# A weight block's low part written by two GpSimd instructions of half the block

## Chip, core and metric

The kernel runs on one core of one Trainium2 chip. The metric is the device time of one launch in microseconds (us), taken as the median of several runs. Engines are named as the profile names them: PE is TensorE's matmul, PEld its weight load, DVE VectorE, ACT ScalarE, POOL GpSimd, SP SyncE.

## What is computed

Two transformer-like blocks run one after the other on 1024 tokens of width 1024, all in float32. Cut to what matters:

```
h    = rms_norm(x) * (1 + sc1) + sh1                 # sc1, sh1 from c @ w_ada
p_u, p_v, p_q, p_k, p_val, p_qi, p_ki, p_wi = split(h @ w_in)
y_a  = spatial_gating(gelu(p_u), gelu(p_v))
y_b  = attention over the 256 keys of highest index score (top-k per query)
x    = x + g1 * rms_norm(concat(norm(y_a), norm(y_b)) @ w_out)
x    = x + g2 * rms_norm(square(relu(h2 @ w_ff1)) @ w_ff2)
...
z    = rms_norm(x) @ w_in_2                          # second block
y_a  = rwkv7_time_mix(z_mix);  y_b = s5_ssm(u)       # a recurrence, a state space
x    = x + (g_a * y_a + g_b * y_b) @ w_out_2
x    = x + square(relu(rms_norm(x) @ w_ff_up_2)) @ w_ff_down_2
return rms_norm(x)
```

## The kernel before, in words

Float32 precision is kept by splitting each operand of a large matmul in two float32r parts: `hi`, the rounded value, and `lo`, what is left. A product is then three matmuls (`mm3`, L66, L68 and L69): hi by hi, and the two mixed ones. So every weight that is loaded needs a `hi` and a `lo` before PE can use it.

`load_w` (L99) does that for one block of weights of 512 KB: one DMA on SP's queue brings it as `wraw` (128 partitions by `nk` row tiles by `n` columns, 1024 elements per partition in 410 blocks and 656 in 8), and `split` (L58) makes `hi` with a copy on ACT (L60) and `lo` with a subtraction on POOL (L61). Both lie in one tile `whl`. Three buffers of `wraw` and three of `whl` let the loads run ahead of PE. Two callers stream the blocks: `token_major` (two row tiles of 512 columns per block) and `feature_major` (four row tiles of 256 columns per block); `merge` calls it directly. The two products that need `lo` of the weights stand at L68 in `token_major` and at L69 in `feature_major`.

The order of each engine's instructions is fixed at build time: the framework's scheduler simulates the program in time and issues by priority. `urgent()` (L53) puts the splits and the reading out of PSUM first. Beside the large matmuls run the parts that live on DVE: the top-k selection (`topk_steps`, a loop of 31 counting steps per tile of 128 queries: the count at L665, one small step at L675 and one at L676 that combines two small tiles in SBUF), the attention (L731 to L775), the triangular solve of the recurrence (L1383 and L1385, 62 short operations per tile), the sums of the feed-forward part (L898). Index scores are made by PE at L631 and L632 from queries that DVE has split (L604), PE has transposed (L124, out of the tile `smr`).

Of the kernel before, what the change touches and what calls it, by code (L numbers as in the profile page):

```python
# [8 lines left out]
F32 = mybir.dt.float32  # L9
# [5 lines left out]
OP = mybir.AluOpType  # L15
# [19 lines left out]
class Kernel:  # L35
# [64 lines left out]
    def load_w(self, w, k0, nk, c0, n, spare=None):  # L100


        nc = self.nc
        for _ in range(2):
            next(self.background, None)
        raw = self.wraw.tile([P, 1024], F32, name="wraw")[:, :nk * n].rearrange("p (k n) -> p k n", n=n)
        nc.sync.dma_start(raw, w[k0 * P:(k0 + nk) * P, c0:c0 + n].rearrange("(k p) n -> p k n", p=P))
        if spare:
            hls = [spare.tile([P, 2, 512], F32R, name="hT") for k in range(nk)]
            for k, hl in enumerate(hls):  # L110
                self.split(hl[:, 0], hl[:, 1], raw[:, k, :])
            return [(hl[:, 0], hl[:, 1]) for hl in hls]
        hl = self.whl.tile([P, 2, 1024], F32R, name="whl")[:, :, :nk * n].rearrange("p a (k n) -> p a k n", n=n)
        self.split(hl[:, 0], hl[:, 1], raw)
        return [(hl[:, 0, k, :], hl[:, 1, k, :]) for k in range(nk)]

    def after(self, n, steps):
# [1749 lines left out]
```

## Time and profile before

| what | value |
|---|---|
| median of 3 runs | 3100.45 us (3094.46 to 3101.99) |
| profiled execution, own time | 3100.2 us |
| its span, first to last instruction | 3098.5 us |
| mean granted TensorE clock | 0.956 of full |
| PE / PEld busy | 92% / 76% |
| DVE / ACT / POOL busy | 59% / 40% / 44% |
| HBM traffic over the span | 119 GB/s |

Outside the span lie 1.7 us. The profiled execution stands 0.25 us under the median, so a sum made against it can be held against the median as it is. PE is the busiest engine in every stretch of the program; its idle time and the time at half clock are what is left to be had.

### The profile page before, as it was taken

Reading aid. Unit: us, or ns where it says so; the run is one execution under the profiler, and the core shown is the slowest. Engines: PE = TensorE matmul, PEld = TensorE weight load, DVE = VectorE, ACT = ScalarE, POOL = GpSimd, SP = SyncE. Lnnn points to the kernel's source line nnn. Section 1 sums busy time; section 2 is a strip of 40 time slices with the busy share of each in tenths; the row PEclk is TensorE's granted clock in tenths of the full one; section 3 lists DMA queues with packets and bytes.
Section 4 is the critical chain, followed back from the end, with each engine's and each line's share of the span. In section 5 each row is a group of like instructions: output and inputs, shape, how many; then the busy total and the mean of one; then the engine's idle time right before and its main releaser. Section 6 shows DMA issues by size and latency. Waiting matters only on the chain. (4 is left out here: it accounts for less than half of the span.)

```text
span 3098.5 us, 41775 instructions
## 1 busy us (share of the span) xinstructions
PE 2841.5 (92%) x15600; PEld 2342.0 (76%) x15600; DVE 1815.0 (59%) x3752; ACT 1249.3 (40%) x2123; POOL 1351.0 (44%) x867
## 2 busy tenths in 40 slices
PE   6977988898999898889899899998999999999998
PEld 5766777687787777668777778877777778888887
DVE  5699679999955944455573455533655643442222
ACT  4545555443444433334233334342343333343333
POOL 4565554443345643333333354442333434454444
PEclk9988999999999999999899999999999999999999
DMA  7445331222224455333224574653323234433332
GB/s 249 124 153 162 123 123 59 86 68 72 65 89 146 167 167 148 109 86 87 74 83 128 151 242 140 164 164 113 96 76 92 85 91 143 148 126 100 99 99 82
DMA packets 301499, 370.18 MB, mean 119 GB/s; under 512 B 70936, under 2 KB 209902, under 8 KB 301040
## 3 DMA queue, kind: packets, MB, share of 16 engines
q1 hardware_dynamic: 293296, 351.75, 37.3%
q10 hardware_dynamic: 8000, 15.76, 1.5%
q8 instruction: 123, 2.02, 0.3%
q14 instruction: 80, 0.66, 0.1%
HBM read 315.80 MB, written 51.65 MB: 119 GB/s over the span
## 5 line engine op out<-in xcount | busy, mean ns | idle before, releaser
L61 POOL TENSOR_TENSOR whl<-wraw,whl 128x1024 fp32r<-128x1024 f32 (+1 forms) x418 | 1025.2, 2460 | 1308.7 <-ACT whl L60 1221.3
L66 PE MATMUL mm<-hT,whl 128*128 128x512 f32 x1760 | 703.0, 400 | 29.2 <-DVE T L1385 5.7
L68 PE MATMUL mm<-hT,whl 128*128 128x512 f32 x1760 | 705.0, 401 | 0.0
L69 PE MATMUL mm<-hT,whl 128*128 128x512 f32 x1760 | 694.7, 398 | 4.7 <-POOL whl L61 4.7
L60 ACT CAST whl<-wraw 128x1024 fp32r<-128x1024 f32 (+1 forms) x418 | 434.8, 1042 | 609.1 <-PE mm L69 436.6
L66 PE MATMUL mm<-whl,hT 128*128 128x512 f32 (+1 forms) x1584 | 609.2, 402 | 50.4 <-DVE acc L898 28.0
L68 PE MATMUL mm<-whl,hT 128*128 128x512 f32 (+1 forms) x1584 | 625.6, 398 | 1.8 <-POOL whl L61 1.8
L69 PE MATMUL mm<-whl,hT 128*128 128x512 f32 (+1 forms) x1584 | 614.6, 397 | 0.4 <-DVE hT L61 0.4
L66 PEld LDWEIGHTS mm<-hT,whl 128*128 128x128 f32 x1760 | 337.2, 192 | 105.2 <-issue 13.4
L66 PEld LDWEIGHTS mm<-whl,hT 128*128 128x128 f32 x1584 | 305.8, 194 | 120.1 <-DVE acc L898 33.0
L69 PEld LDWEIGHTS mm<-hT,whl 128*128 128x128 f32 x1760 | 338.2, 192 | 75.9 <-POOL whl L61 6.4
L68 PEld LDWEIGHTS mm<-hT,whl 128*128 128x128 f32 x1760 | 337.9, 192 | 67.2 <-issue 0.9
L68 PEld LDWEIGHTS mm<-whl,hT 128*128 128x128 f32 x1584 | 306.1, 193 | 62.5 <-POOL whl L61 2.3
L69 PEld LDWEIGHTS mm<-whl,hT 128*128 128x128 f32 x1584 | 304.4, 193 | 62.1 <-DVE hT L61 1.0
L61 DVE TENSOR_TENSOR hT<-sm,hT 128x512 fp32r<-128x512 f32 x112 | 130.9, 1173 | 277.4 <-ACT hT L60 276.4
L898 DVE TENSOR_TENSOR acc<-mm,acc 128x512 f32<-128x512 f32 x240 | 162.2, 687 | 173.0 <-PE mm L69 172.8
L665 DVE TENSOR_SCALAR_CACHE_REDUCE junk<-score,topk 128x640 uint8<-128x640 f32 (+4 forms) x192 | 180.0, 940 | 1.8
L877 ACT ACTIVATE sm<-mm 128x512 f32<-128x512 f32 x128 | 76.5, 597 | 165.0 <-PE mm L69 163.6
L1383 DVE TENSOR_TENSOR Ttmp<-L,T 128x60 f32<-128x60 f32 (+24 forms) x248 | 78.4, 316 | 90.9 <-DMA L<-lt_d 83.5
L60 ACT CAST hT<-sm 128x512 fp32r<-128x512 f32 x144 | 89.4, 621 | 32.2 <-DVE sm L1831 28.7
L676 DVE SCALAR_TENSOR_TENSOR topk<-topk,topk 128x1 int32<-128x1 int32 x186 | 86.7, 469 | 1.3
L739 ACT ACTIVATE p<-p,nm 128x128 f32<-128x128 f32 (+7 forms) x64 | 49.5, 775 | 91.5 <-DVE nm L735 66.2
(471 smaller groups left out, 3495.3 us busy)
## 6 DMA issues: line engine op xcount, KB each, us to landing
wraw<-w_ff SPq DMA_DIRECT2D x128, 512.0 KB
wraw<-w_in SPq DMA_DIRECT2D x100, 512.0 KB
wraw<-w_ff_up SPq DMA_DIRECT2D x64, 512.0 KB
wraw<-w_ff_down SPq DMA_DIRECT2D x64, 512.0 KB
wraw<-w_ada SPq DMA_DIRECT2D x32, 512.0 KB
wraw<-w_out SPq DMA_DIRECT2D x32, 512.0 KB
raw<-w_ada SPq DMA_DIRECT2D x16, 512.0 KB
x_d<-acc ACTq DMA_DIRECT2D x16, 512.0 KB
```

Source lines behind the costliest of these rows:

```text
L60: self.nc.scalar.copy(hi, src)
L61: (engine or self.nc.gpsimd).tensor_tensor(lo, src, hi.bitcast(F32), op=OP.subtract)
L66: nc.tensor.matmul(ps, a[0], b[0], start=start, stop=False)
L68: nc.tensor.matmul(ps, a[0], b[1], start=False, stop=False)
L69: nc.tensor.matmul(ps, a[1], b[0], start=False, stop=stop)
L665: V.tensor_scalar(junk[:, :n], sel, value, 0.0, op0=op, op1=OP.add, accum_out=cnt)
L676: V.scalar_tensor_tensor(u, t, (1 << b) ^ (1 << b >> 1), keep, op0=OP.bitwise_xor, op1=OP.bitwise_xor)
L739: nc.scalar.activation(p[:, :n], p[:, :n], AF.Exp, bias=nm, scale=0.125, accum_out=su)
L877: nc.scalar.activation(r, ps, AF.Relu)
L898: nc.vector.tensor_tensor(d, pss[j], d, op=OP.add)
L1383: V.tensor_tensor(tmp[:, :n, :w], L[:, j:j + 1, j + 1:].to_broadcast([P, n, w]), T[:, :n, j:j + 1].to_broadcast([P, n, w]), op=OP.mult)
```

## The change

The branch of `load_w` that serves nearly all weights no longer calls `split`. It keeps the one ACT copy of the whole block and issues the subtraction as two POOL instructions, the first for the lower half of the row tiles, the second for the upper half. The branch for the last four tiles (`spare`) and all other splits stay.

```diff
         hl = self.whl.tile([P, 2, 1024], F32R, name="whl")[:, :, :nk * n].rearrange("p a (k n) -> p a k n", n=n)
-        self.split(hl[:, 0], hl[:, 1], raw)
+
+        with self.urgent():
+            nc.scalar.copy(hl[:, 0], raw)
+            for s in (slice(0, nk // 2), slice(nk // 2, nk)):
+                nc.gpsimd.tensor_tensor(hl[:, 1, s], raw[:, s], hl[:, 0, s].bitcast(F32), op=OP.subtract)
         return [(hl[:, 0, k, :], hl[:, 1, k, :]) for k in range(nk)]
```

Lines behind this place stand four lines lower in the changed kernel: L124 is then L128, L631 is L635, L898 is L902. The subtraction of a weight block is L118 there. The number of instructions is the same on every engine, but for the 418 further subtractions on POOL and two activation-table loads on ACT that fall away (30 instead of 32). The scheduler sees the two shorter subtractions, and so it moves other instructions.

On POOL, in the first feed-forward part beside the top-k selection (`whl` is a weight block, `hT` the feed-forward's activations, `smr` a split key tile), before:

```order
L582 TENSOR_TENSOR smr<-smS,smr 128x2x64
L583 COPY smr<-smr 128x2x64
L61 TENSOR_TENSOR whl<-wraw,whl 128x1024
L61 TENSOR_TENSOR hT<-sm,hT 128x512
L61 TENSOR_TENSOR whl<-wraw,whl 128x1024
L582 TENSOR_TENSOR smr<-smS,smr 128x2x64
L61 TENSOR_TENSOR hT<-sm,hT 128x512
L583 COPY smr<-smr 128x2x64
L61 TENSOR_TENSOR whl<-wraw,whl 128x1024 x5
```

and with the change:

```order
L586 TENSOR_TENSOR smr<-smS,smr 128x2x64 x2
L61 TENSOR_TENSOR hT<-sm,hT 128x512
L587 COPY smr<-smr 128x2x64 x2
L118 TENSOR_TENSOR whl<-wraw,whl 128x512 x2
L61 TENSOR_TENSOR hT<-sm,hT 128x512
L118 TENSOR_TENSOR whl<-wraw,whl 128x512 x2
L61 TENSOR_TENSOR hT<-sm,hT 128x512
L118 TENSOR_TENSOR whl<-wraw,whl 128x512 x10
```

The two halves of a block always stand next to each other; nothing of POOL's other work comes between them.

On PE, at the start of the product with `w_out` (`mm` with `hT` and `whl`), where the transposes of the next index-score queries (`tp` out of `smr`) are woven in, before:

```order
L66 MATMUL mm<-hT,whl 128x512
L68 MATMUL mm<-hT,whl 128x512
L124 MATMUL tp<-ident,smr 128x128 x8
L69 MATMUL mm<-hT,whl 128x512
L66 MATMUL mm<-hT,whl 128x512
```

and with the change, from the product's beginning on:

```order
L128 MATMUL mm<-ident,acc 128x128 x24
L66 MATMUL mm<-hT,whl 128x512
L68 MATMUL mm<-hT,whl 128x512
L69 MATMUL mm<-hT,whl 128x512
L66 MATMUL mm<-hT,whl 128x512
L128 MATMUL tp<-ident,smr 128x128 x4
L68 MATMUL mm<-hT,whl 128x512
L69 MATMUL mm<-hT,whl 128x512
```

Before, 26 matmuls of the product stood ahead of the eight transposes; now 4 stand ahead of the first four and 10 ahead of the last four. The index scores of the four tiles that follow (L631, now L635) move with them, 15 to 27 matmuls forward against the stream of the large product. Elsewhere the shift has the other sign: the attention of both halves stands mostly 10 to 26 matmuls later, the recurrence's last two tiles 19 to 25 matmuls later, with the distances inside each tile kept to within 5.

## Rows read from the trace of the kernel before

**Rows 1.** The page's busy time, share of the span and instructions of each engine.

```profile
PE 2841.5 (92%) x15600; PEld 2342.0 (76%) x15600; DVE 1815.0 (59%) x3752; ACT 1249.3 (40%) x2123; POOL 1351.0 (44%) x867
```

**Rows 2.** Windows: PE, PEld, DVE, ACT, POOL busy us (instructions), clock, DMA share, GB/s.

```profile
100.00:900.00 800.00, 707.46 (x3414) 587.72 (x3413) 707.50 (x1758) 385.06 (x735) 390.74 (x278) 0.94 0.32 101
900.00:2600.00 1700.00, 1571.08 (x9664) 1286.21 (x9663) 904.29 (x1726) 639.11 (x1041) 686.46 (x412) 0.96 0.42 124
2600.00:3098.00 498.00, 489.63 (x2177) 405.44 (x2175) 152.51 (x176) 183.61 (x267) 224.61 (x118) 1.00 0.35 113
...
2800.00:2900.00 100.00, 100.00 (x443) 82.79 (x442) 23.79 (x27) 36.39 (x48) 42.94 (x18) 1.00 0.31 97
```

**Rows 3.** POOL's subtractions: busy us, mean ns, idle before; then min/median/max ns.

```profile
L61 POOL TENSOR_TENSOR whl<-wraw,whl 128x1024 fp32r<-128x1024 f32 x410 | 1012.2, 2476 | 1301.6 <-ACT whl L60 1214.3 <-issue 53.9 <-PE tp L1322 12.5
...
L61 POOL TENSOR_TENSOR whl<-wraw,whl x418: 1588/2397/4412, 23.2 to 3067.9; 128x1024 fp32r<-128x1024 f32 x138, 128x656 fp32r<-128x656 f32 x2
L61 POOL TENSOR_TENSOR hT<-sm,hT x32: 1279/1302/1754, 495.7 to 945.9; 128x512 fp32r<-128x512 f32 x32
```

**Rows 4.** Waits of all engines, then PE's: us in total, times, longest.

```profile
ACT whl L60 <- PE mm L69: 436.6, 147, 17.0
...
PE tp L1401 <- DVE TI L1397: 42.2, 9, 11.2
PE mm L66 <- DVE acc L898: 33.5, 11, 8.1
PE mm L69 <- POOL whl L61: 4.7, 4, 2.3
PE mm L68 <- POOL whl L61: 1.8, 2, 1.1
```

**Rows 5.** POOL's timeline near 575 us: start us, us, what.

```profile
572.97 2.41 POOL L61 TENSOR_TENSOR whl<-wraw,whl 128x1024 fp32r<-128x1024 f32 x1
...
578.28 2.34 POOL L61 TENSOR_TENSOR whl<-wraw,whl 128x1024 fp32r<-128x1024 f32 x1 [1.01 <-ACT whl L60]
```

**Rows 6.** DVE's timeline over the same stretch.

```profile
574.54 0.84 DVE L676 SCALAR_TENSOR_TENSOR topk<-topk,topk 128x1 int32<-128x1 int32 x1
...
578.22 0.88 DVE L665 TENSOR_SCALAR_CACHE_REDUCE junk<-score,topk 128x640 uint8<-128x640 f32 x1
...
579.02 1.62 DVE L676 SCALAR_TENSOR_TENSOR topk<-topk,topk 128x1 int32<-128x1 int32 x1
```

**Rows 7.** DVE's L676: min/median/max ns; then its group's busy us and mean ns.

```profile
L676 DVE SCALAR_TENSOR_TENSOR topk<-topk,topk x186: 132/155/2355, 127.8 to 841.1; 128x1 int32<-128x1 int32 x186
...
L676 DVE SCALAR_TENSOR_TENSOR topk<-topk,topk 128x1 int32<-128x1 int32 x186 | 86.7, 469 | 1.3
```

**Rows 8.** Windows of line 61 alone: DVE's and POOL's busy us, 100 to 900 us.

```profile
100.00:900.00 800.00, 0.00 (x0) 256.86 (x120) 0.94 0.32 101
```

**Rows 9.** Timelines of POOL and DVE near 661 us: two blocks back to back.

```profile
660.21 4.78 POOL L61 TENSOR_TENSOR whl<-wraw,whl 128x1024 fp32r<-128x1024 f32 x2 [6.48 <-ACT whl L60]
...
661.20 1.43 DVE L676 SCALAR_TENSOR_TENSOR topk<-topk,topk 128x1 int32<-128x1 int32 x1
```

**Rows 10.** Timelines of DVE, POOL and PE near 1481 us, in the recurrence's solve.

```profile
1479.93 0.23 DVE L1385 TENSOR_TENSOR T<-T,Ttmp 128x69 f32<-128x69 f32 x1
...
1480.69 4.66 POOL L61 TENSOR_TENSOR whl<-wraw,whl 128x1024 fp32r<-128x1024 f32 x2 [15.70 <-ACT whl L60]
...
1480.74 2.38 DVE L1383 TENSOR_TENSOR Ttmp<-L,T 128x66 f32<-128x66 f32 x1
...
1483.64 2.27 DVE L1373 TENSOR_TENSOR W<-W,cols 128x512 f32<-128x512 f32 x1
...
1483.77 0.79 PE L66 MATMUL mm<-whl,hT 128*128 128x512 f32 x1 [7.11 <-DVE acc L898]
```

**Rows 11.** Timelines of DVE and PE near 478 us, at the first index-score queries of `w_out`.

```profile
476.14 0.75 DVE L604 TENSOR_TENSOR smr<-smS,smr 128x256 fp32r<-128x256 f32 x2
...
479.97 0.71 PE L124 MATMUL tp<-ident,smr 128*128 128x128 f32 x7
```

## The prediction

> **What bounds the kernel now.** I read the busy time first. PE is busy 92% of the span, POOL 44% [rows 1], so an edit of POOL's work can pay only through what PE waits for. The windows show where PE idles [rows 2]: 92.5 us of the 800 between 100 and 900 us (800 - 707.46), where DVE is busy 88% with the top-k selection and the attention; 128.9 us of the next 1700; 8.4 us of the last 498, where PE runs without a gap at full clock. So what can be won lies ahead of 2600 us, and most densely ahead of 900 us.
>
> Then the waits. The low part of the weights, which the change makes sooner, ends 4.7 + 1.8 = 6.5 us of PE's waits, in six places [rows 4]. The weights run ahead: ACT's copy of a block waits 436.6 us in 147 places for PE to free a `whl` buffer [rows 4], and POOL is idle 1301.6 us ahead of its subtractions, 1214.3 of them waiting for that copy [rows 3]. The longest PE waits are DVE's: 42.2 us for the recurrence's transposed solve, 33.5 us for the feed-forward sums [rows 4].
>
> Last the timelines, for what POOL does to DVE. At 572.97 us POOL starts a subtraction of 2.41 us, which ends at 575.38; DVE's L676, a step on one column, starts at 574.54, takes 0.84 us and ends at 575.38 as well. The next one of POOL runs from 578.28 to 580.62; L676 starts at 579.02, takes 1.62 us, ends at 580.64 [rows 5, 6]. Its median over 186 is 0.155 us, its longest 2.355, its mean 0.469 [rows 7]. So this DVE step, which reads two operands from SBUF, stands still until POOL's subtraction is over, while the count L665 runs through beside it in 0.88 us [rows 6]. **That hold, not the wait for weights, is what two shorter instructions may shorten.**
>
> **The change, part by part.**
>
> *The first half is ready sooner.* A subtraction of 1024 elements has a median of 2.397 us, one of 512 elements 1.302 [rows 3]. The first half ends 1.1 us earlier than the whole did. Where PE waits for it, the gain is at most the 6.5 us of these waits and at least nothing, since PE may next need the second half. I take -3 us, the middle, as some of these waits are for the first row tile.
>
> *More POOL work.* Two halves take 2 x 1.302 = 2.604 us, 0.207 more than the whole. Over 418 blocks that is 87 us: POOL rises from 1351 to some 1440 us, 46%. It is hidden by POOL's own idle time ahead of these subtractions, and by the two further buffers that PE still has to work through when a third is being split: ACT's copies wait for PE, not PE for them [rows 4]. The second half is 0.2 us later than before. If this cover were gone, six waits would grow by 0.2 us each, 1.2 us. I take 0. The `wraw` buffer is free 0.2 us later, and the load behind it on SP's queue starts as much later; three such buffers cover that, so 0 as well.
>
> *DVE is held for a shorter time.* For the top-k step the excess is 186 x (0.469 - 0.155) = 58 us [rows 7]. Between 100 and 900 us the weight blocks and the like at L61 are 256.86 of POOL's 390.74 busy us [rows 2, 8]; the rest, which the change leaves alone, holds DVE just so. So some 58 x 0.66 = 38 us stem from subtractions at L61. How much of a hold goes depends on which engine gets its turn when the first half ends. Near 661 us two whole subtractions stand back to back, 4.78 us from 660.21; L676 starts at 661.20 and ends at 662.63, when the first is over (660.21 + 2.39 = 662.60), not at 664.99 with the second [rows 9]. DVE gets in between. After the change a held step then waits at most for one half, 1.3 us less its own 0.15; the next L676 comes after one count (0.88 us or more) and two small steps, when the second half is nearly over. With arrivals spread evenly over the loop, a hold that was 1.6 us becomes 0.7 with both halves counted: a bit over half is saved, 0.6 x 38 = 23 us of DVE's time.
>
> Of DVE's time PE sees only what lies right ahead of one of its waits. PE's share of idle in this stretch is 11.6%, DVE's 11.6% too: they limit it in turns. I take 0.4 of the 23 us, -9 us. The bounds: all of it, -23 us; and, if DVE gets no turn between halves (below), +10 us.
>
> The Trainium skill, page "SBUF — State Buffer", section "Who interferes with whom", puts such holds down to a port pair that a DVE instruction with two SBUF inputs and a GpSimd instruction take exclusively, each for its whole length. By that rule each half is a lock of its own, and DVE may hold POOL off between them; rows 9 agree for two whole subtractions. Where DVE issues such instructions densely, the rule gives no gain at all, and I give that as a rival.
>
> *The clock.* From 100 to 900 us the granted clock is 0.94, in the last stretch 1.00 [rows 2]: 6% of 800 us are 48 us of clock. A tenth less idle (9 of 92.5) should give back up to a tenth, 5 us; I take -2, with 0 and -5 as ends.
>
> *The moved instructions.* Two table loads less on ACT lie on an engine with 40% busy: 0. On PE the index scores stand up to 27 matmuls earlier, the attention 10 to 26 later, both against the same stream, at 100/443 = 0.226 us a matmul [rows 2] some 4 to 6 us each way. Later is slack ahead of a wait, earlier is slack lost, and both are paid once per stretch, not at every step. In the recurrence the distance from the masked products to L1401 is kept to within 5 matmuls, 1.1 us, so its 42.2 us stay. I take 0 for the sum of these, with -10 and +20 as ends (the upper one is the third rival).
>
> **The sum:** -3 + 0 - 9 - 2 + 0 = -14 us. Against the profiled execution's 3100.2 us that is **3086 us**, and as that execution lies 0.25 us under the median, the same against the median: 0.45% faster. What a measurement of this kernel can tell from no change is about 0.3%, 9.3 us.
>
> **The rivals.**
>
> *A. Both halves are paid (no change).* In the triangular solve DVE issues two-input steps one behind the other, 0.23 us each. At 1480.74 us L1383 is held for 2.38 us, and L1373 at 1483.64 for 2.27, by the two subtractions that run from 1480.69 to 1485.35; PE then waits 7.11 us for the sum behind them [rows 10]. With halves, DVE would get one short step in between and be held again: 2.6 us in place of 2.4. If the loop of the top-k also meets the second half in full, the 58 us of holds, some 26 of 2.2 us, each grow by 0.2 us, 5 us of DVE's time, and twice that with the solve's: the +10 us above, of which 0.4 reach PE. With the -3 of the first part and nothing else: 3100 + 4 - 3 = 3101 us. For it: the solve's rows. Against it: the count L665 that lies between two steps of the loop [rows 6].
>
> *B. The order costs more than the halves give (slower).* The first index-score queries of the `w_out` product are transposed at 479.97 us without a wait; DVE had split them at 476.14 + 0.75 = 476.89 [rows 11]. So 3.1 us were in hand. With 22 and 16 matmuls less ahead of them, PE comes there 5.0 and 3.6 us earlier, and waits up to 1.9 us; at 24 matmuls, 5.4 us, and four tiles, that is (5.4 - 3.1) x 4 = 9 us, and as much again if each gap is followed by a stretch at half clock. It decides from the point where less than 14 matmuls (3.1 us) stay ahead of the transposes, as they do in the new order. If the holds give back little: 3100 - 3 + 18 = 3115 us. Against it: DVE's own order puts this branch's steps earlier too, and faster top-k steps help the same queue.
>
> *C. The gain comes in full.* All 23 us of DVE, all 6.5 of the first halves, 5 of clock: 3100 - 34 = 3066 us. For it: where DVE alone is late, each us of it is one of the span, and it is busy as long as PE there [rows 2]. Against it: PE has to do its 707 us there too.
>
> *D. PE still waits for both halves.* Then the first term falls and the others stay: 3089 us, within my forecast's own range.
>
> **How the numbers follow.** Forecast, with D: 0.45 (3072 to 3091). A: 0.28. B: 0.20. C: 0.07. The range takes in forecast, A and most of B and C: 3064 to 3116 us; a little under 2 in 10 lies outside. Faster by over 0.3% (below 3091): 0.45 + 0.07 = 0.52, less what of the forecast's spread falls short, 0.50. Slower by over 0.3% (above 3109.8): B and a little of A, 0.21. Between: 0.29.
>
> **What would show it.** Right: halves near 1.3 us on POOL, POOL busy near 1440 us; L676's longest near 1.3 us and its mean near 0.3; PE's idle time between 100 and 900 us down from 92.5 to some 80; the six waits for `whl` nearly gone; the recurrence's waits of 42 us as they were. Wrong: L676's longest still above 2 us (A); new PE waits for `smr` or for L635's PSUM tiles between 450 and 600 us (B); PE's gaps unchanged though DVE's busy time falls by 20 us, which would mean that DVE's holds were never on the path.

## The result, and the profile after

The changed kernel takes 3054.04 us (median of 4 runs, 3047.99 to 3063.16) against 3100.57 us of the kernel before on the same chip (4 runs): the ratio is 0.9863, with a 95% interval of 0.9842 to 0.9883. That is 46.5 us or 1.4% faster, where 14 us had been forecast. The direction held, the size did not, and the time lies 10 us below the lower end of the range. The profiled execution after is the slowest of its four, 3063.16 us, 9 us above the median; its own distance to the profiled execution before is 37 us.

The busy row of the changed kernel's page, which answers to [rows 1]:

```profile
PE 2831.0 (92%) x15600; PEld 2337.1 (76%) x15600; DVE 1745.7 (57%) x3752; ACT 1245.3 (41%) x2121; POOL 1460.9 (48%) x1285
```

DVE does the same 3752 instructions in 69 us less, and POOL is busy for 110 us more. PE's busy time falls by 10 us with the same 15600 matmuls, and the mean granted clock rises from 0.956 to 0.960 of full.

Its windows, cut where the program stands at 100, 900 and 2600 us before, as near as the changed order allows (columns as in [rows 2]):

```profile
100.00:877.00 777.00, 697.82 (x3412) 582.11 (x3411) 684.10 (x1759) 386.64 (x732) 409.47 (x368) 0.95 0.33 104
877.00:2563.00 1686.00, 1568.57 (x9660) 1285.22 (x9660) 875.12 (x1726) 635.11 (x1040) 748.40 (x640) 0.96 0.43 125
2563.00:3061.00 498.00, 489.60 (x2177) 405.51 (x2175) 137.18 (x176) 181.04 (x267) 249.99 (x203) 0.99 0.35 112
```

The first stretch is 23 us shorter, the second 14 us, the last not at all. DVE's busy time falls in all three.

POOL's subtractions and DVE's L680 (L676 before), as groups and by their durations; these answer to [rows 3, 7]:

```profile
L118 POOL TENSOR_TENSOR whl<-wraw,whl 128x512 fp32r<-128x512 f32 (+1 forms) x836 | 1134.7, 1382 | 1255.7 <-ACT whl L116 1187.1 <-issue 62.8 <-DMA sm<-gate_d 4.4
...
L118 POOL TENSOR_TENSOR whl<-wraw,whl x836: 884/1292/3312, 23.2 to 3033.1; 128x512 fp32r<-128x512 f32 x164, 128x328 fp32r<-128x328 f32 x4
...
L680 DVE SCALAR_TENSOR_TENSOR topk<-topk,topk 128x1 int32<-128x1 int32 x186 | 75.5, 410 | 1.4
...
L680 DVE SCALAR_TENSOR_TENSOR topk<-topk,topk x186: 144/159/4205, 123.1 to 810.6; 128x1 int32<-128x1 int32 x186
```

A half takes 1.292 us in the median, 1.382 in the mean of all pieces. L680's mean is 0.410 us, not the 0.3 that was forecast, and its longest 4.2 us. How one hold looks now is seen in the timeline, POOL's row first, then DVE's:

```profile
779.66 2.56 POOL L118 TENSOR_TENSOR whl<-wraw,whl 128x512 fp32r<-128x512 f32 x2
...
779.53 0.15 DVE L679 TENSOR_SCALAR topk<-topk 128x1 int32<-128x1 f32 x1
779.72 1.25 DVE L680 SCALAR_TENSOR_TENSOR topk<-topk,topk 128x1 int32<-128x1 int32 x1
781.01 1.28 DVE L669 TENSOR_SCALAR_CACHE_REDUCE junk<-score,topk 128x1024 uint8<-128x1024 f32 x1
```

Two halves run from 779.66 to 782.22. L680 starts at 779.72 and ends at 780.97, when the first half is over (779.66 + 1.29 = 780.95). The count L669 then goes through beside the second half.

PE's longest waits for DVE, which answer to the second and third of [rows 4]:

```profile
PE tp L1405 <- DVE TI L1401: 42.7, 8, 9.5
PE mm L66 <- DVE acc L902: 31.9, 8, 7.6
```

They are what they were. PE's idle time over the span falls from 257 us (3098.5 - 2841.5) to 230 (3061.4 - 2831.0), so these 27 us lie in other, mostly shorter waits; the other 10 us of the 37 are PE's busy time.

### The profile page after: what moved, and what is told of

Its sections match the earlier page's. It is cut to its first block, busy times and chain, and to the rows that moved or that the text cites. A ratio compares the mean times of both kernels' runs of the same rounds, so it can differ in the third digit from the quotient of the medians.

```text
span 3061.4 us, 42378 instructions
## 1 busy us (share of the span) xinstructions
PE 2831.0 (92%) x15600; PEld 2337.1 (76%) x15600; DVE 1745.7 (57%) x3752; ACT 1245.3 (41%) x2121; POOL 1460.9 (48%) x1285
## 4 chain that ended last, share of the span: by engine, by line
PE 57%; DVE 27%; DMA 8%; issue 3%; ACT 2%; SPq 2%; POOL 1%; ACTq 0%; POOLq 0%; DVEq 0%
PE mm L66 16%; PE mm L68 16%; PE mm L69 16%; DVE junk L669 4%; DMA L<-lt_d 3%; DVE T L1389 2%; DVE Ttmp L1387 2%; DVE topk L680 2%; PE tp L128 1%; DVE acc L902 1%; DVE score L643 1%; DVE p L746 1%; DMA TT<-tt_d 1%; DVE p L735 1%; PE tp L764 1%
## 5 line engine op out<-in xcount | busy, mean ns | idle before, releaser
L118 POOL TENSOR_TENSOR whl<-wraw,whl 128x512 fp32r<-128x512 f32 (+1 forms) x836 | 1134.7, 1382 | 1255.7 <-ACT whl L116 1187.1
L69 PE MATMUL mm<-hT,whl 128*128 128x512 f32 x1760 | 694.8, 397 | 3.9 <-POOL whl L118 3.9
L66 PE MATMUL mm<-whl,hT 128*128 128x512 f32 (+1 forms) x1584 | 614.6, 402 | 42.9 <-DVE acc L902 18.5
L69 PE MATMUL mm<-whl,hT 128*128 128x512 f32 (+1 forms) x1584 | 614.3, 396 | 0.9 <-DVE hT L61 0.9
L69 PEld LDWEIGHTS mm<-hT,whl 128*128 128x128 f32 x1760 | 336.3, 191 | 73.7 <-POOL whl L118 5.0
L69 PEld LDWEIGHTS mm<-whl,hT 128*128 128x128 f32 x1584 | 303.3, 192 | 62.2 <-DVE hT L61 1.8
L902 DVE TENSOR_TENSOR acc<-mm,acc 128x512 f32<-128x512 f32 x240 | 160.6, 686 | 189.2 <-PE mm L69 188.7
L61 DVE TENSOR_TENSOR hT<-sm,hT 128x512 fp32r<-128x512 f32 x112 | 94.4, 846 | 265.2 <-ACT hT L60 264.5
L669 DVE TENSOR_SCALAR_CACHE_REDUCE junk<-score,topk 128x640 uint8<-128x640 f32 (+4 forms) x192 | 179.5, 941 | 1.8
L764 PE MATMUL tp<-pT,vhl 128*128 128x256 f32 x288 | 64.1, 310 | 25.0 <-ACT pT L760 7.4
```

What stands on the lines that cost most here:

```text
L61: (engine or self.nc.gpsimd).tensor_tensor(lo, src, hi.bitcast(F32), op=OP.subtract)
L66: nc.tensor.matmul(ps, a[0], b[0], start=start, stop=False)
L69: nc.tensor.matmul(ps, a[1], b[0], start=False, stop=stop)
L118: nc.gpsimd.tensor_tensor(hl[:, 1, s], raw[:, s], hl[:, 0, s].bitcast(F32), op=OP.subtract)
L669: V.tensor_scalar(junk[:, :n], sel, value, 0.0, op0=op, op1=OP.add, accum_out=cnt)
L764: nc.tensor.matmul(o, self.vhl[(s0 + i) // 4][:, (s0 + i) % 4, kv, :], t[:, x, 256 * i:256 * i + 256], start=(s0 + i + x == 0), stop=(s0 + ...
```

## The experiments

Three theories stood against each other. **H**: DVE is held for a shorter time by POOL's running subtraction. **F**: the first half of a block is ready sooner. **O**: the scheduler's new order of the instructions on all engines. To separate them, most kernels below are issued in a given order: the program is built once as before, the order of each engine is read off, and the changed program is tied to it, a block's pieces standing where the whole stood. The part of the code that does so:

```diff
+            for k in order:
+                for i in by.pop(k[:3], []):
+                    if k[0] in last:
+                        tc.add_manual_dep(i, last[k[0]].name, behind, reason="order")
+                    last[k[0]] = i
```

"Old order" means that of the kernel before. Lines are those of the changed kernel, but the subtraction is L117 (L119 in the last two runs). Ratios are to the kernel before on the same chip, with 95% intervals.

**1. Halves in the old order.** The change alone, without what the scheduler made of it.

```diff
+def halves(nk):
+    return [slice(0, nk // 2), slice(nk // 2, nk)]
...
+    order = whole
+    nc, _ = program(arrays, halves, order and program(arrays, order)[1])
```

> The subtractions are split into halves as in the change, but every engine issues its instructions in the order of the kernel before (the two halves stand where the whole stood). Theory H (DVE is held for a shorter time): the gain stays, 3045 to 3065 us; DVE's total busy time some 60 to 70 us below the kernel before, PE's idle time some 20 to 30 us below it. Theory O (the gain comes from the new order of instructions): it is gone, 3095 to 3105 us, although DVE is busy for some 60 us less. In between, say 3075 us: both carry a part.

Measured: 3045.85 us, ratio 0.9835 (0.9815 to 0.9855). The whole gain is there. Its busy row:

```profile
PE 2823.0 (93%) x15600; PEld 2334.0 (77%) x15600; DVE 1723.0 (57%) x3752; ACT 1251.3 (41%) x2123; POOL 1457.1 (48%) x1285
```

DVE is busy for 92 us less than before, not the 60 to 70 that were expected, and PE is idle for 38 us less (257 to 3041.9 - 2823.0 = 219), not 20 to 30.

**2. Whole subtractions in the new order.**

```diff
+    order = halves
+    nc, _ = program(arrays, whole, order and program(arrays, order)[1])
```

> The counterpart: whole subtractions, but every engine issues in the order of the changed kernel. Theory H: no gain, 3095 to 3110 us, DVE's busy time as in the kernel before (1815 us). Theory O: the gain is here, 3045 to 3065 us.

Measured: 3090.84 us, ratio 0.9992 (0.9976 to 1.0009). Its busy row:

```profile
PE 2841.1 (92%) x15600; PEld 2340.4 (76%) x15600; DVE 1827.1 (59%) x3752; ACT 1244.9 (40%) x2121; POOL 1346.3 (44%) x867
```

DVE is as busy as before (1827.1 against 1815.0). The time lies a little below the range for H, but so does the kernel before on this chip, with 3096.53 us. O falls: the order alone is worth less than 0.3% either way, although it stands 15 to 27 matmuls off in places.

**3. Halves reversed**, the upper half first, old order.

```diff
+def reverse(nk):
+    return halves(nk)[::-1]
```

> Halves in the order of the kernel before, but the upper half of a block is subtracted first, the lower half second, so the row tiles that PE needs first are ready 0.2 us later than with a whole subtraction, not 1.1 us sooner. Theory F (the first half is ready sooner, and that is the gain): it falls back to 3095 to 3105 us. Theory H: within 5 us of the run with halves in the same order of instructions.

Measured: 3048.27 us, ratio 0.984 (0.9823 to 0.9856), against 0.9835 with the halves the right way round. PE's wait L69 for the block's low part is 2.5 us in run 1 and 4.7 here:

```profile
PE mm L69 <- POOL whl L117: 2.5, 2, 2.1
```

```profile
PE mm L69 <- POOL whl L117: 4.7, 3, 2.2
```

By these waits F is worth some 2 us, and the two times, 2.4 us apart, can't tell it from nothing. H is left: in the same order of instructions, only the length of POOL's pieces differs. Runs 8 and 10 test it by other edits.

**4. Quarters**, old order.

```diff
+    return [(s, c) for s in (slice(0, nk // 2), slice(nk // 2, nk)) for c in (slice(0, n // 2), slice(n // 2, n))]
```

> Four subtractions of a quarter of the block each, 256 elements, in the order of the kernel before. Theory H, with DVE getting its turn after each piece: the longest hold falls from some 1.1 to some 0.6 us, DVE's busy time by another 20 to 40 us, and the time by another 5 to 20 us below the run with halves, 3030 to 3055 us. Rival P (the added start-up time of POOL's pieces is paid, each piece takes the port again): DVE's busy time does not fall further, and the time is that of the halves or up to 15 us above it; POOL rises to some 1600 us.

Measured: 3037.41 us, ratio 0.9807 (0.9788 to 0.9825).

```profile
PE 2827.2 (93%) x15600; PEld 2338.2 (77%) x15600; DVE 1672.2 (55%) x3752; ACT 1251.8 (41%) x2123; POOL 1619.2 (53%) x2121
```

DVE's busy time falls by another 51 us (1723.0 in run 1), more than expected, the time by only 8, and the intervals of the two ratios overlap.

**5 and 6. Where the gain arises**: halves in the first 104 blocks, ahead of 900 us, and in the other 314 alone.

```diff
+    return [slice(0, nk // 2), slice(nk // 2, nk)] if b < 104 else [slice(0, nk)]
```

```diff
+    return [slice(0, nk // 2), slice(nk // 2, nk)] if b >= 104 else [slice(0, nk)]
```

> Order of the kernel before; only the first 104 blocks of weights, those subtracted ahead of 900 us in the kernel before, are split into halves, the other 314 stay whole. The forecast's reading (what can be won lies where DVE is busy 88%, ahead of 900 us) gives here the whole gain of the halves, some 45 to 50 us, 3045 to 3055. By the lead of the changed kernel's events over those of before, only some 19 to 24 us arise there: 3070 to 3080 us. If the forecast's own sum of 14 us was right for this stretch: 3080 to 3086.

> The counterpart: the first 104 blocks whole, the 314 after them in halves. The forecast's reading: no gain, 3092 to 3100 us. The lead of the events: 20 to 30 us, 3067 to 3077 us. If the gains add up, this and the run before together give the gain of all halves, some 50 us.

Measured: 3061.8 us, ratio 0.9888 (0.9855 to 0.9922), and 3080.88 us, 0.9954 (0.9938 to 0.997). So 1.1% and 0.5%, together 1.6%, the 1.65% of all halves: the gains add up. The stretch ahead of 900 us alone is worth some 35 us (24 to 45), more than the changed kernel's profiled execution had led me to expect. Neither time lies in one of the ranges that were written down: more arises ahead of 900 us than the events' lead said, less than all of it.

**7. A microsecond of DVE's time**: one step of the top-k is issued twice.

```diff
-            V.tensor_scalar(keep, cnt, 256.0, float(1 << b), op0=OP.is_ge, op1=OP.mult)
+            self.subs.append([V.tensor_scalar(keep, cnt, 256.0, float(1 << b), op0=OP.is_ge, op1=OP.mult).ins.name for _ in range(1 if self.before else 2)])
```

`self.before` is true in the build from which the order is read.

> What is a microsecond of DVE worth ahead of 900 us? Whole subtractions and the order of the kernel before; the top-k's step on one column (L675 before, one SBUF operand, 0.147 us, never held) is issued twice in each of the 186 rounds: 186 x 0.147 = 27 us more of DVE's time between 127 and 841 us and nothing else. The forecast's factor of 0.4: 11 us, a time some 8 to 14 us above the kernel before. If DVE's chain alone sets the pace there (factor 0.9 to 1, as the halves ahead of 900 us suggest: DVE 39 us less busy, the end 32 us earlier): 22 to 30 us above it.

Measured: 3121.0 us, ratio 1.0093 (1.0062 to 1.0125): 29 us more (19 to 39) for 27 us of steps. The factor of 0.4 falls. It was not "nothing else", though: DVE's busy time rises by 19 us only, from 1815.0 to 1834.1, since some other steps are held less.

**8. The held step with one SBUF tensor**, whole subtractions, old order.

```diff
-            V.scalar_tensor_tensor(u, t, (1 << b) ^ (1 << b >> 1), keep, op0=OP.bitwise_xor, op1=OP.bitwise_xor)
+            (V.scalar_tensor_tensor if self.before else V.tensor_scalar)(u, t, (1 << b) ^ (1 << b >> 1), keep, op0=OP.bitwise_xor, op1=OP.bitwise_xor)
```

> Whole subtractions, order of the kernel before; the held step of the top-k (L676 before, L680 here) is written as a tensor_scalar whose second operand comes as a per-partition scalar, so that it has one SBUF tensor to read in place of two. Theory H in its sharp form (only DVE instructions with two SBUF tensors, or a fast form, are held): the step takes 0.15 us each time, DVE is busy for some 55 us less between 127 and 841 us, and the time falls by 35 to 55 us if that chain sets the pace there, by some 20 to 25 us with the factor 0.4. Rival (every DVE instruction that meets a running subtraction is held, whatever its form, or the hold moves on to the next step): L680's longest stays above 2 us or the next step's becomes so, and the time stays within 8 us of the kernel before.

Measured: 3062.75 us, ratio 0.9911 (0.988 to 0.9943). L680 by its durations:

```profile
L680 DVE TENSOR_SCALAR topk<-topk,topk x186: 186/208/217, 127.8 to 807.6; 128x1 int32<-128x1 int32 x186
```

Not one of 186 is held, though 39 of them start beside a whole subtraction that runs on for 0.3 us or more. POOL's work and order are as before and the new form is no faster when nothing holds it, so here the freed holds alone make the gain: with runs 1 to 3, H is shown. The gain, some 28 us by the ratio, is smaller than the 35 to 55 expected, and so is what DVE is relieved of: 35 us (1815.0 to 1780.3), not 55. The new form takes 208 ns against 155 [rows 7], 10 us for 186, and other steps are now held in its place: L604 (L608 here) goes from a mean of 733 to one of 932 ns.

```profile
L604 DVE TENSOR_TENSOR smr<-smS,smr 128x256 fp32r<-128x256 f32 x28 | 20.1, 733 | 13.5 <-ACT smr L603 13.5
```

```profile
L608 DVE TENSOR_TENSOR smr<-smS,smr 128x256 fp32r<-128x256 f32 x28 | 25.7, 932 | 13.7 <-ACT smr L607 13.7
```

**9. Eighths**, old order.

```diff
+    return [(s, slice(c, c + n // 4)) for s in (slice(0, nk // 2), slice(nk // 2, nk)) for c in range(0, n, n // 4)]
```

> Eight subtractions of 128 elements for each block, order of the kernel before. Theory H goes on: longest hold by a block some 0.4 us, another 3 to 10 us less than with quarters, 3027 to 3035 us. Rival P (POOL's start-up of each piece adds up: some 8 x 0.45 us = 3.6 us a block in place of 2.4, and DVE meets a running piece more often): no gain over quarters or 3 to 15 us lost, 3037 to 3052 us; POOL busy for 1750 us or more.

Measured: 3034.77 us, ratio 0.9812 (0.9778 to 0.9847). In us that is the upper end of H's range, but the ratio is no better than that of quarters, as the rival has it.

```profile
PE 2824.7 (93%) x15600; PEld 2330.8 (77%) x15600; DVE 1624.4 (53%) x3752; ACT 1252.2 (41%) x2123; POOL 1896.9 (62%) x3793
...
L680 DVE SCALAR_TENSOR_TENSOR topk<-topk,topk x186: 138/186/9365, 122.4 to 804.4; 128x1 int32<-128x1 int32 x186
```

DVE is busy for 48 us less than with quarters, and it does not help. POOL is busy for 278 us more, and one hold of L680 lasts 9.4 us: DVE did not get its turn at every joint between two pieces. PE's waits that grow, first with quarters, then with eighths:

```profile
PE mm L69 <- POOL whl L117: 2.5, 2, 1.8
PE mm L68 <- POOL whl L117: 0.4, 1, 0.4
```

```profile
PE tp L128 <- DVE topk L679: 9.5, 1, 9.5
PE mm L69 <- POOL whl L117: 6.9, 7, 2.7
PE mm L68 <- POOL whl L117: 6.0, 6, 1.8
```

The waits for the block's low part rise from 2.9 to 12.9 us, and the wait of 9.5 us ends at 567.79, behind the hold of L680 from 554.78 to 564.15.

**10. Quarters, and the modulation's additions in pieces** of 256 columns, old order.

```diff
-                    nc.gpsimd.tensor_tensor(acc, acc, raw, op=OP.add)
+                    for c in range(0, D, 256):
+                        nc.gpsimd.tensor_tensor(acc[:, c:c + 256], acc[:, c:c + 256], raw[:, c:c + 256], op=OP.add)
```

> Quarters as before, and the 28 additions of 128x1024 that POOL does for the modulation (L437, 2.4 us each, between 100 and 350 us and on) cut into four pieces of 256 columns too. Theory H, which is about any long instruction of POOL and not about weights: DVE's busy time falls by another 10 to 25 us, the longest hold of L680 falls from 2.25 us to below 1.3 us, the time by 3 to 10 us, 3027 to 3034 us. If only the weight blocks mattered: that of the quarters, 3034 to 3040 us.

Measured: 3022.09 us, ratio 0.9776 (0.9736 to 0.9817), against 0.9807 with quarters alone; the intervals overlap.

```profile
L680 DVE SCALAR_TENSOR_TENSOR topk<-topk,topk x186: 139/228/1251, 124.1 to 788.3; 128x1 int32<-128x1 int32 x186
```

L680's longest falls to 1.25 us as expected: the holds above 1.4 us that were left after the change all stand beside these additions of 2.4 us, which it leaves whole. The longest, 4.2 us, met two of them, in the changed kernel:

```profile
160.25 2.38 POOL L437 TENSOR_TENSOR adac<-adac,wraw 128x1024 f32<-128x1024 f32 x1
162.55 0.30 POOL L587 CAST smr<-smr 128x128 fp32r<-128x128 f32 x1
162.80 2.35 POOL L437 TENSOR_TENSOR adac<-adac,wraw 128x1024 f32<-128x1024 f32 x1
...
160.97 4.21 DVE L680 SCALAR_TENSOR_TENSOR topk<-topk,topk 128x1 int32<-128x1 int32 x1
```

**11 and 12. Versions to keep**, in the scheduler's own order: run 10 without a forced order, and that with the edit of run 8.

> The version to keep: blocks in quarters and the modulation's additions in pieces of 256 columns as in the run before, but nothing forces the order, the scheduler arranges it. Theory H with no part for the order: as with the forced order, ratio 0.978, 3020 to 3040 us. If the order matters for such short pieces: off by more than 15 us either way.

> The two cures together, in the scheduler's own order: blocks and modulation sums in pieces of 256, and the top-k's step with one SBUF operand. With the quarters alone that step still loses 186 x its excess, some 40 us of DVE's time; alone the other form gave 33 us of 49 back, since other steps were held in its place. Theory H: a further 5 to 20 us, 2998 to 3014 us. If the quarters have already taken DVE off the path that sets the end: within 5 us of the quarters, 3014 to 3024 us.

Measured: 3018.65 us, ratio 0.9769 (0.9741 to 0.9797), and 2995.19 us, ratio 0.9692 (0.9663 to 0.9722). The second edit brings another 0.8%, some 24 us, a little over the 5 to 20 expected. The last kernel is faster than that before and that with the change; against the 0.9863 of the change it is another 1.7%. Its busy row:

```profile
PE 2804.6 (94%) x15600; PEld 2321.2 (78%) x15600; DVE 1637.8 (55%) x3752; ACT 1246.8 (42%) x2119; POOL 1630.4 (55%) x2205
```

## Why the direction was right and the size wrong

**What a microsecond of DVE is worth: this step failed.** The prediction put it as "Of DVE's time PE sees only what lies right ahead of one of its waits [...] they limit it in turns. I take 0.4 of the 23 us, -9 us." In the runs with the old order the stretch of [rows 2] from 100 to 900 us holds the same 1758 instructions of DVE, 1944 with the doubled step. Its bounds are the starts of the same instructions. The windows of runs 1, 3, 4, 5, 8, 9, 10 and 7, one fence each:

```profile
99.00:862.30 763.30, 696.00 (x3414) 583.50 (x3413) 674.71 (x1758) 386.68 (x735) 409.18 (x369) 0.95 0.34 105
862.30:2543.50 1681.20, 1563.11 (x9664) 1281.55 (x9663) 868.35 (x1726) 639.50 (x1041) 748.03 (x639) 0.96 0.43 125
2543.50:3041.90 498.40, 489.59 (x2177) 405.40 (x2175) 130.58 (x176) 183.60 (x267) 248.03 (x204) 0.99 0.35 113
```

```profile
99.40:867.00 767.60, 699.62 (x3414) 586.33 (x3413) 668.92 (x1758) 386.76 (x735) 409.51 (x369) 0.94 0.33 105
```

```profile
98.60:861.00 762.40, 697.89 (x3414) 585.63 (x3413) 659.60 (x1758) 387.26 (x735) 445.19 (x552) 0.94 0.34 105
```

```profile
100.10:868.20 768.10, 702.57 (x3413) 589.47 (x3412) 669.26 (x1758) 386.65 (x735) 409.37 (x368) 0.94 0.32 105
```

```profile
99.90:867.10 767.20, 698.94 (x3413) 587.01 (x3412) 674.28 (x1758) 385.72 (x735) 392.66 (x278) 0.94 0.33 105
```

```profile
93.80:863.50 769.70, 695.56 (x3413) 581.63 (x3412) 657.92 (x1758) 387.81 (x735) 507.43 (x919) 0.95 0.32 104
```

```profile
97.20:846.80 749.60, 696.40 (x3414) 584.80 (x3413) 648.30 (x1758) 386.79 (x735) 459.19 (x636) 0.95 0.33 107
```

```profile
100.40:924.10 823.70, 714.95 (x3413) 592.05 (x3413) 726.03 (x1944) 385.14 (x735) 392.18 (x278) 0.93 0.30 98
```

Worked out from these rows (idle is the stretch less busy):

| run | stretch us | DVE busy | DVE idle | PE idle |
|---|---|---|---|---|
| before [rows 2] | 800.0 | 707.5 | 92.5 | 92.5 |
| 1 halves | 763.3 | 674.7 | 88.6 | 67.3 |
| 3 halves reversed | 767.6 | 668.9 | 98.7 | 68.0 |
| 4 quarters | 762.4 | 659.6 | 102.8 | 64.5 |
| 5 halves ahead of 900 us | 768.1 | 669.3 | 98.8 | 65.5 |
| 8 one operand | 767.2 | 674.3 | 92.9 | 68.3 |
| 9 eighths | 769.7 | 657.9 | 111.8 | 74.1 |
| 10 quarters, sums | 749.6 | 648.3 | 101.3 | 53.2 |
| 7 doubled step | 823.7 | 726.0 | 97.7 | 108.7 |

With whole subtractions and with halves the stretch is as long as DVE is busy, plus 89 to 99 us, while DVE's busy time goes from 726 to 669 us. PE's idle time gives way, from 109 to 66 us. So DVE sets the pace there, and most of its 92.5 us of idle time is no slack but what its own chain spends in waiting for its partners. In run 1 the stretch loses 36.7 us for 32.8 of DVE, a factor of 1.1; in run 7 it grows by 23.7 for 18.5, 1.3; in runs 3, 5 and 8 it is 0.8 to 1.0. With smaller pieces DVE's idle time grows, to 101 to 103 us with quarters and 112 with eighths, and the factor is 0.8 and 0.9 in runs 4 and 10 and 0.6 in run 9: run 4 relieves DVE of 15 us more than run 1, and the stretch ends 1 us sooner. Run 9 shows two waits of PE that grow; what takes up the rest stays open.

The equal idle shares of both engines, from which I read that they limit in turns, could not tell this: the length of a stretch less the busy time of an engine is slack only if it shrinks when that engine gets slower. Windows of 100 us in the trace of the kernel before would have told more (columns as in [rows 2]):

```profile
200.00:300.00 100.00, 77.97 (x344) 64.20 (x345) 96.80 (x294) 47.40 (x103) 56.60 (x44) 0.81 0.53 170
500.00:600.00 100.00, 83.78 (x363) 66.68 (x364) 99.46 (x240) 43.78 (x83) 44.57 (x33) 0.93 0.26 77
```

DVE is busy for 97 and 99% there and PE for 78 and 84%, so PE is not the busiest engine in every stretch, as the section on time and profile before has it.

**What DVE is relieved of: the sum was too small.** I counted L676 alone, 23 us. In run 1 its mean goes from 469 [rows 7] to 380 ns, 186 x 0.089 = 16.5 us:

```profile
L680 DVE SCALAR_TENSOR_TENSOR topk<-topk,topk 128x1 int32<-128x1 int32 x186 | 70.2, 380 | 1.3
```

That term came out a little smaller. But DVE as a whole gains 32.8 us in this stretch. The other half is spread over many steps, none with more than 4 us; some 9 us of it lie in steps with one SBUF tensor (below). In the changed kernel itself L680 gives 186 x 0.059 = 11 us and DVE as a whole 23.4 (707.5 to 684.1 in its first window). That this equals the 23 us of the forecast is luck: half of it comes from steps that the sum did not have.

**Where it can be won.** "So what can be won lies ahead of 2600 us, and most densely ahead of 900 us", the prediction says, but its sum had no term for DVE behind 900 us. Run 1 gains 18.8 us from 900 to 2600 (1700 to 1681.2) for 35.9 of DVE (904.29 to 868.35), a factor of 0.5, and nothing in the last stretch, 498.0 to 498.4, for 21.9 of DVE. With PE busy 88%, 92% and 98% in the three [rows 2], a microsecond of DVE is worth 1.1, 0.5 and 0 in run 1, and 36.7 + 18.8 - 0.4 us make 55 of the 56 us that its profiled execution gains. Most of what DVE gains in the later two, 38 of 58 us, lies in L61, the feed-forward's own splits, which the prediction did not count; before, and in run 1:

```profile
L61 DVE TENSOR_TENSOR hT<-sm,hT 128x512 fp32r<-128x512 f32 x112 | 130.9, 1173 | 277.4 <-ACT hT L60 276.4
```

```profile
L61 DVE TENSOR_TENSOR hT<-sm,hT 128x512 fp32r<-128x512 f32 x112 | 92.8, 832 | 288.7 <-ACT hT L60 288.0
```

**The clock.** I took -2 us with -5 as the end. In run 1 the same 3414 matmuls from 100 to 900 us keep PE busy for 696.0 in place of 707.46 us, at a granted clock of 0.95 against 0.94, and the next 9664 for 1563.1 in place of 1571.1. So 19 of the 56 us of that execution (3098.5 to 3041.9 us of span) are PE's busy time, and as the matmuls are the same, I put them down to the clock. They are a part of the gains above and not beside them: of the 36.7 us ahead of 900 us, 11.5 are busy time, where -2 was forecast, and 25.2 are idle time, 0.8 of DVE's 32.8, where 0.4 was forecast.

**What was right.** That shorter holds of DVE make the gain. The first half: -3 us forecast, some 2 by run 3's waits, too little for its time to show. More POOL work: 1460.9 us on POOL, 21 above the forecast; no price of it shows with halves, though one does with eighths. The moved instructions: 0 forecast, 0.9992 in run 2. The recurrence's 42 us stayed, and PE's idle time in the first stretch came to 79.2 us (777.0 - 697.82), where some 80 had been forecast. Rival C, "each us of it is one of the span", had the mechanism; it got 0.07, and was itself too small.

**Rivals and signs.** Rival A falls: DVE is let in between halves. Its sign, L680's longest above 2 us, came all the same, from the modulation's additions, and so was no sign of A. The wait of 7.11 us that stood for A in [rows 10] lies behind the first hold alone: the sum L898 runs from 1483.04 to 1483.72, and L1373, the second held step, follows it. The waits for `whl` are not nearly gone, as was forecast; they fall from 6.5 us to 3.9 + 0.4 in the changed kernel. Rival B falls with run 2.

**Which instructions are held.** The Trainium skill, page "SBUF — State Buffer", section "Who interferes with whom", says in its second point that a DVE instruction with at most one SBUF input does not contend, outside the 2-port perf modes. Run 8 agrees: 217 ns at most against 2355 before [rows 7], and the second operand that came as a scalar counted for nothing. But one SBUF tensor is not enough to be free of holds. L742 is a tensor_scalar with one SBUF tensor too, of 256 columns; others of its shape take 0.34 us. In the kernel before, POOL's row first:

```profile
243.97 2.40 POOL L61 TENSOR_TENSOR whl<-wraw,whl 128x1024 fp32r<-128x1024 f32 x1
...
244.07 2.44 DVE L742 TENSOR_SCALAR p<-p,rsu 128x256 f32<-128x256 f32 x1
```

It is held until the subtraction is over. Whether it ran in such a mode, no run here tells.

## What to carry to other kernels

Cost a hold of DVE by every instruction that is seen held beside a long POOL instruction, not by the one that shows it best, and price a microsecond of it by the stretch: where making DVE slower makes the stretch longer by as much, the factor is one. Cut POOL's long elementwise work into pieces; here 256 elements did as well as 128. Where DVE has a small frequent step that is held, try a form with one SBUF tensor and see in the trace whether the hold goes. An order imposed on the rebuilt program separates an edit from what a scheduler makes of it.

## What the runs showed of the hardware

DVE's turn between two POOL instructions that follow at once is usual, not certain. Take as let in a DVE instruction that was held up to such a joint and ends within its own shortest duration and 0.1 us of it. By the starts and ends in the traces, DVE was let in at 190 of 191 such joints in run 1, at 281 of 281 in run 4 and at 343 of 389 with eighths, where 33 of the 46 others fall to two holds of L680, of 9.4 and 7.1 us. So it is not lost now and then at a single joint, but mostly in rare spells at all of them. In run 11 one L682 waits 8.11 us, while ten POOL instructions pass, POOL's rows first:

```profile
544.82 1.30 POOL L61 TENSOR_TENSOR hT<-sm,hT 128x512 fp32r<-128x512 f32 x1
546.07 5.62 POOL L119 TENSOR_TENSOR whl<-wraw,whl 128x256 fp32r<-128x256 f32 x8
551.62 1.30 POOL L61 TENSOR_TENSOR hT<-sm,hT 128x512 fp32r<-128x512 f32 x1
...
544.83 8.11 DVE L682 SCALAR_TENSOR_TENSOR topk<-topk,topk 128x1 int32<-128x1 int32 x1
```

What decides the turn stays open; no run was made for it. With eighths one such hold stands ahead of a PE wait of 9.5 us (run 9), a part of why the shortest pieces did not pay.
